# Attention with whole probabilities and a difference of value blocks; score maxima and final roots computed with per-partition scalar columns

## The chip, the cores and the metric

One NeuronCore of a Trainium2 chip runs the whole program. TensorE (PE) does the matrix products and PE transposes, VectorE (DVE) and ScalarE (ACT) work on PSUM and SBUF, GpSimd (POOL) on SBUF, and SyncE (SP) issues the transfers. The metric is device time in microseconds from launch to end; lower is better.

## The reference

A two-layer decoder trunk over 1024 tokens of width 1024. Layer 0 mixes by pooling windows and a short convolution. Layer 1, which the change touches, is sliding-window attention with 16 query heads, 2 key/value heads, a learned sink per head, and blocks of 128 queries. A final RMSNorm follows.

```python
# window 128, blocks of 128 queries; each block sees its own and the previous block of keys
band = (diff >= 0) & (diff < WINDOW)            # diff = i + 128 - j
scores = einsum("bnqkgd,bnskd->bnkgqs", qb, kb) * scale
...
m = maximum(max(scores, -1), sink)
p = exp(scores - m)
p = p / (sum(p, -1) + exp(sink - m))
out = einsum("bnkgqs,bnskd->bnqkgd", p, vb)     # vb = [previous block, own block]
...
h = h + (out * silu(z)) @ w_out + b_out
return h * rsqrt(mean(h * h) + 1e-5) * final_norm_g
```

With a window of 128 and blocks of 128, a query at row i sees exactly 128 keys: the keys j <= i of its own block and the keys j > i of the block before. One 128 x 128 tile of probabilities per head and block thus holds everything: on and below the diagonal stand the own block's keys, above it those of the block before.

## The kernel before

All products are split into a high part (fp32r) and a low rest, so most things exist twice (h and lo, H and L). `split` does that: ACT casts, DVE (or POOL) subtracts.

Layer 0 and the projections of layer 1 run first. The attention then runs as a loop over blocks, `for b in range(NB + 1)`, each with two halves `js` of 8 heads, and the halves of three blocks overlap in it:

- `values(b)` splits block b's values (`vtok[:, b, :]`, in SBUF) into `vp[b]`.
- `queries(b + 1, js)`: ACT casts and POOL subtracts (L936), PE transposes (L939), ACT copies to `qT` (L941).
- `probs(b, js)`: for two groups g of four heads, PE transposes the probabilities `pts` into a PSUM bank (L1058), `split` makes `curH` and `curL` (ACT L179, DVE L180, tile pT), and for b > 0 POOL makes masked copies: `affine_select` L1064 writes the previous block's part to new tiles, L1067 keeps the own block's part in place. That is four selects per group, eight per half.
- `scores(b + 1, js, qT)`: four steps `pair`, each with two heads: PE scores into a bank (L960, L961), DVE merges the two blocks (L966), takes the maxima of both heads (L968), and turns them into the two biases of the exponentials (L969); ACT takes the two exponentials (L972). After the last pair, `norm` computes the sink's part and the reciprocal (L978 to L981) and POOL scales the probabilities (L983).
- `project(b - 1, js)`: 24 products per half with the output weights (L1113 to L1115); the four score steps are spread among them. `summed` adds the residual (L1146), squares (ACT L1147) and multiplies by the final gain (POOL L1150).
- `attend(b, js)`: products of values and probabilities (L1081; for b > 0 eight per half), then ACT L1088, DVE L1089 and L1092, and `split` into aH and aL.
- `finish(b - 1)`: `rsqrt_mean` with n == 1 works on one column: two tensor_scalar (L138), a first guess (L141), and three rounds of L145 and L149, then ACT scales the block (L1129) and it is stored. Its instructions run in the DVE's row during the next block's half js = 0.

PE's order is the program's order. The order on DVE, ACT, POOL and SP in this stage is the one that the scheduler of the language works out at build time. The PSUM banks of scores, transposed queries and transposed probabilities come from one rotation of four buffers (psB).

Of the kernel before, what the change touches and what calls it, by code (L numbers as in the profile page):

```python
# [9 lines left out]
F32 = mybir.dt.float32  # L10
F32R = mybir.dt.float32r
# [3 lines left out]
ALU = mybir.AluOpType  # L15
# [3 lines left out]
P = 128  # L19
# [6 lines left out]
HD = 64  # L26
# [6 lines left out]
WARM = 8  # L33
W_BUFS = 9
T3_BUFS = 14
LEAD = 3
AHEAD = 6
ZLATE = 6
# [40 lines left out]
def trunk(ctx, tc, x, xT, g1, pos, cols, w_in, w_pool, w_out, w_q, w_kv, w_z, b_q, b_kv,  # L79
               sinks, w_o, g_fin, out):  # L80
    nc = tc.nc
    mm, tr = nc.tensor.matmul, nc.tensor.transpose
    act = nc.scalar.activation
    tt, stt, ts = nc.vector.tensor_tensor, nc.vector.scalar_tensor_tensor, nc.vector.tensor_scalar
    ptt = nc.gpsimd.tensor_tensor
# [15 lines left out]
    def psB(dtype=F32):  # L101
# [17 lines left out]
                            compare_op=ALU.is_gt, fill=0.0, base=0, channel_multiplier=-1)  # L119
# [9 lines left out]
    def rsqrt_mean(pool, out_ap, sums, n, part=None):  # L129


        v = pool.tile([P, 8], F32, name="rs_v", bufs=2)[:, :n]
        y = pool.tile([P, 8], F32, name="rs_y", bufs=2)[:, :n]
        a = pool.tile([P, 8], F32, name="rs_a", bufs=2)[:, :n]
        if n == 1:
            h = pool.tile([P, 1], F32, name="rs_h", bufs=2)
            for dst, c in ((v, 1.0), (h, -0.5)):
                ts(out=dst, in0=sums, scalar1=part, scalar2=c / D, op0=ALU.add, op1=ALU.mult)  # L138
        else:
            ts(out=v, in0=sums, scalar1=1.0 / D, scalar2=EPS, op0=ALU.mult, op1=ALU.add)  # L140
        ts(out=y.bitcast(I32), in0=v.bitcast(I32), scalar1=-0.5, scalar2=float(0x5F3759DF),  # L141
           op0=ALU.mult, op1=ALU.add)
        for it in range(3):
            if n == 1:
                stt(out=a, in0=y, scalar=h, in1=y, op0=ALU.mult, op1=ALU.mult)  # L145
            else:
                tt(out=a, in0=y, in1=y, op=ALU.mult)
                stt(out=a, in0=a, scalar=-0.5, in1=v, op0=ALU.mult, op1=ALU.mult)
            stt(out=out_ap if it == 2 else y, in0=a, scalar=1.5, in1=y, op0=ALU.add, op1=ALU.mult)  # L149

    def diag_r(rcol, s):

# [25 lines left out]
    def split(dst_h, dst_l, src, sub=tt):  # L178
        nc.scalar.copy(out=dst_h, in_=src)  # L179
        sub(out=dst_l, in0=src, in1=dst_h.bitcast(F32), op=ALU.subtract)  # L180
# [65 lines left out]
    nsink = const.tile([P, NH], F32, name="nsink")  # L246
# [129 lines left out]
    wraw, wsum, whl, at = {}, {}, {}, {p: i for i, p in enumerate(prods)}  # L376
# [343 lines left out]
    for g in range(4):  # L720
        src = u_pair(g)
        for j in (2 * g, 2 * g + 1):
            if j % 2 and g:
                gated(g, src)
            v = ch_pair(j)
# [20 lines left out]
    if True:  # L746
# [41 lines left out]
        for s in range(2):  # L788
            acc = t2()
            for m in range(8):  # L790
# [5 lines left out]
                for kh in range(2):  # L796
                    w = take()
                    for k in range(KT):
                        f = 8 * kh + k
# [5 lines left out]
                if s == 0 and m == 7:  # L805
# [3 lines left out]
                h, lo = big2(s, F32R), big2(s, F32R)  # L809
                act(out=h, in_=h1, func=AF.Copy, scale=col(C_G2, m))  # L810
                stt(out=lo, in0=h1, scalar=col(C_G2, m), in1=h.bitcast(F32), op0=ALU.mult,
                    op1=ALU.subtract)
# [31 lines left out]
    vtok = keep.tile([P, NB, P], F32, name="vtok")  # L844
# [5 lines left out]
    with tc.tile_pool(name="l1", bufs=2, reuse_waits="tile") as p1:  # L850
# [24 lines left out]
        for b in range(NB):  # L875
            if b + 3 < NB:
# [4 lines left out]
                in1=bkv[:, 0:P], op0=ALU.mult, op1=ALU.add)  # L881
            stt(out=vtok[:, b, :], in0=dst[:, P:256], scalar=rcol1[:, b:b + 1],
                in1=bkv[:, P:256], op0=ALU.mult, op1=ALU.add)
# [13 lines left out]
        for c in range(2):  # L897
            wq = [p for _ in range(4) for p in take(0)]
            for b in range(NB):
# [6 lines left out]
                if c == 0 and 0 < b < 5 or c == 1 and b == 5:  # L906
# [3 lines left out]
                    in1=bq[:, hs(c)], op0=ALU.mult, op1=ALU.add)  # L910
# [34 lines left out]
    def scores(b, js, qT):  # L945

        cols_ = slice(8 * js, 8 * js + 8)
        smax = pe.tile([P, 8], F32, name="smax")
        den = pe.tile([P, 8], F32, name="den")
        res = [pe.tile([P, 4, P], F32, name=f"pt{js}", bufs=2) for _ in range(2)]  # L950
        um = umask.to_broadcast([P, 2, P])

        def pair(g, i2):
            bank = psB()
            bv = bank.rearrange("p (h c) -> p h c", c=256)
            at = 4 * g + 2 * i2
            for i in range(2):
                lq = qT[g][:, (2 * i2 + i) * P:(2 * i2 + i + 1) * P]
                lo, dst = (0, bv[:, i, P:256]) if b == 0 else ((b - 1) * P, bv[:, i, :])
                mm(dst, lhsT=lq, rhs=kT[:, 2 * g, lo:(b + 1) * P], start=True, stop=False)  # L960
                mm(dst, lhsT=lq, rhs=kT[:, 2 * g + 1, lo:(b + 1) * P], start=False, stop=True)  # L961
            if b == 0:
                nc.vector.copy_predicated(out=bv[:, :, P:256], mask=um,
                                          data=neg.unsqueeze(1).to_broadcast([P, 2, P]))
            else:
                nc.vector.copy_predicated(out=bv[:, :, P:256], mask=um, data=bv[:, :, 0:P])  # L966
            m = smax[:, at:at + 2]
            nc.vector.tensor_reduce(out=m, in_=bv[:, :, P:256], axis=AX.X, op=ALU.max)  # L968
            stt(out=m, in0=m, scalar=-0.125, in1=nsink[:, 8 * js + at:8 * js + at + 2],  # L969
                op0=ALU.mult, op1=ALU.min)  # L970
            for i in range(2):
                exps.append(act(  # L972
                    out=res[g][:, 2 * i2 + i, :], in_=bv[:, i, P:256], func=AF.Exp, scale=0.125,
                    bias=smax[:, at + i:at + i + 1], accum_out=den[:, at + i:at + i + 1]))

        def norm():
            es = pe.tile([P, 8], F32, name="es")
            tt(out=es, in0=sink[:, cols_], in1=smax, op=ALU.add)  # L978
            act(out=es, in_=es, func=AF.Exp)
            tt(out=es, in0=den, in1=es, op=ALU.add)  # L980
            nc.vector.reciprocal(out=es, in_=es)  # L981
            for g in range(2):
                ptt(out=res[g], in0=res[g],  # L983
                    in1=es[:, 4 * g:4 * g + 4].unsqueeze(2).to_broadcast([P, 4, P]), op=ALU.mult)

        def last():
            pair(1, 1)
            norm()

        return res, [lambda: pair(0, 0), lambda: pair(0, 1), lambda: pair(1, 0), last]  # L990


# [48 lines left out]
    pa = ctx.enter_context(tc.tile_pool(name="pa", bufs=2, reuse_waits="tile"))  # L1041

    vp = {}

    def values(b):

        t = pa.tile([P, 4, HD], F32R, name="vp", bufs=3)
        v = vtok[:, b, :].rearrange("p (g d) -> p g d", d=HD)
        split(t[:, 0::3, :], t[:, 1:3, :], v)
        vp[b] = t  # L1050

    def probs(b, js):

        terms = []
        for g in range(2):
            bank = psB()
            for i in range(4):
                tr(bank[:, i * P:(i + 1) * P], pts[b, js][g][:, i, :], ident)  # L1058
            curH, curL = (pa.tile([P, 4, P], F32R, name="pT", bufs=9) for _ in range(2))
            split(curH, curL, bank.rearrange("p (h c) -> p h c", c=P))  # L1060
            if b:
                prvH, prvL = (pa.tile([P, 4, P], F32R, name="pT", bufs=9) for _ in range(2))
                for a, t in ((prvH, curH), (prvL, curL)):
                    nc.gpsimd.affine_select(out=a, in_=t.bitcast(F32), pattern=[[0, 4], [-1, P]],  # L1064
                                            compare_op=ALU.is_gt, fill=0.0, base=0,
                                            channel_multiplier=1)
                    nc.gpsimd.affine_select(out=t, in_=t.bitcast(F32), pattern=[[0, 4], [1, P]],  # L1067
                                            compare_op=ALU.is_ge, fill=0.0, base=0,
                                            channel_multiplier=-1)
                terms.append((vp[b - 1], g, prvH, prvL))  # L1070
            terms.append((vp[b], g, curH, curL))
        return terms

    def attend(b, js, terms):
        dst = []
        for g in range(2):
            bank = psA("psA")
            ops = [(v[:, 2 * g:2 * g + 2, :].rearrange("p a d -> p (a d)"), p)
                   for v, gg, h, lo in terms if gg == g for p in (h, lo)]
            for i, (v, p) in enumerate(ops):  # L1080
                mm(bank, lhsT=v, rhs=p, start=(i == 0), stop=(i == len(ops) - 1))  # L1081
            dst.append(bank.rearrange("p (j c) -> p j c", c=P))

        low = pa.tile([P, 4, P], F32, name="pT", bufs=9)
        at = pa.tile([P, 4, P], F32, name="pT", bufs=9)
        for g in range(2):
            own, other = slice(g * HD, (g + 1) * HD), slice((1 - g) * HD, (2 - g) * HD)
            nc.scalar.copy(out=low[own], in_=dst[g][other])  # L1088
            tt(out=at[own], in0=dst[g][own], in1=low[own], op=ALU.add)  # L1089
        s, bb = divmod(b, 4)  # L1090
        for jj in range(2):
            tt(out=at[:, 2 * jj:2 * jj + 2, :], in0=at[:, 2 * jj:2 * jj + 2, :],  # L1092
               in1=sz[4 * s + 2 * js + jj][:, :, bb * P:(bb + 1) * P], op=ALU.mult)
        aH = pa.tile([P, 4, P], F32R, name="aH", bufs=3)
        aL = pa.tile([P, 4, P], F32R, name="aL", bufs=3)
        split(aH, aL, at)
        return aH, aL
# [147 lines left out]
```

## Time and profile before

| what | value |
|---|---|
| median of 3 runs | 1136.29 us (1135.53 to 1137.89) |
| the profiled execution's own time | 1137.09 us |
| its span, first to last instruction | 1135.4 us |
| PE busy | 1078.5 us, 95% |
| DVE busy | 783.5 us, 69% |
| ACT busy | 463.5 us, 41% |
| POOL busy | 224.6 us, 20% |
| granted TensorE clock, mean | 0.995 |

The time is that of the whole launch; the span leaves out 1.7 us around the first and the last instruction. Busy shares are means over the whole program, whose stages differ: the attention loop is the last sixth of it.

### The profile page before, as it was taken

The numbers are of one execution on the slowest core, as the hardware profiler recorded it, in microseconds if no ns is written. First come the engines' busy times: TensorE is split into PE (matmuls) and PEld (weight loads), VectorE is DVE, ScalarE is ACT, GpSimd is POOL, SyncE is SP. The second block draws the span as 40 slices with busy tenths as digits, with TensorE's granted clock in tenths as the row PEclk, the third lists the DMA queues.
The fourth block names the chain that finished last, engine by engine and source line by source line (L and its number), as shares of the span: only waits on it lengthen the run. The fifth ranks groups of instructions, "written<-read, shape, count | busy, mean of one in ns | idle before, by whom it ended". The sixth has DMA issues, their size and how long they took to land.

```text
span 1135.4 us, 14172 instructions
## 1 busy us (share of the span) xinstructions
PE 1078.5 (95%) x5020; PEld 873.1 (77%) x5020; DVE 783.5 (69%) x1392; ACT 463.5 (41%) x961; POOL 224.6 (20%) x396
## 2 busy tenths in 40 slices
PE   4989999999999999999999999999999997898897
PEld 3767788888888888887788788988888885676776
DVE  4699879967696669866645854721143679889995
ACT  4753332423233332334324423320023777777653
POOL 0000000000000000000001010333320226788874
PEclk9999999999999999999999999999999999999999
DMA  5342331221212212126653334410022305370001
GB/s 204 112 167 99 141 128 38 93 84 38 93 38 96 81 56 75 65 75 226 222 203 134 137 142 146 165 38 19 1 93 96 127 24 125 57 93 20 20 20 56
DMA packets 70694, 109.09 MB, mean 96 GB/s; under 512 B 37472, under 2 KB 37600, under 8 KB 70624
## 3 DMA queue, kind: packets, MB, share of 16 engines
q1 hardware_dynamic: 70624, 108.20, 28.9%
q8 instruction: 39, 0.64, 0.2%
q14 instruction: 31, 0.25, 0.1%
HBM read 89.04 MB, written 19.14 MB: 95 GB/s over the span
## 4 chain that ended last, share of the span: by engine, by line
PE 79%; DVE 12%; ACT 5%; issue 2%; DMA 2%; POOL 0%; SPq 0%; DVEq 0%; ACTq 0%
PE b L440 38%; PE psD L801 3%; PE psD L802 3%; PE psA L800 2%; PE psD L800 2%; PE psA L802 2%; PE psA L801 2%; PE psA L186 2%; PE psD L186 2%; PE psA L187 2%; PE psA L188 2%; PE psD L188 2%; PE psD L187 2%; ACT pt L972 1%; DMA W<-w_in 1%
## 5 line engine op out<-in xcount | busy, mean ns | idle before, releaser
L179 ACT CAST W<-W 128x512 fp32r<-128x512 f32 (+1 forms) x199 | 143.9, 731 | 357.9 <-DVE W L180 108.5
L180 DVE TENSOR_TENSOR W<-W 128x512 fp32r<-128x512 f32 (+1 forms) x199 | 162.6, 823 | 115.2 <-ACT W L179 68.6
L690 POOL MEMSET T<- 128x16 f32 x8 | 0.9, 111 | 358.4 <-DVE T L624 229.2
L818 POOL TENSOR_TENSOR t<-t,T 128x512 f32<-128x512 f32 x14 | 19.4, 1387 | 248.5 <-ACT T L817 248.5
L440 PE MATMUL b<-B11h,W 128*128 128x512 f32 x192 | 65.6, 405 | 2.7 <-ACT W L179 1.8
L440 PE MATMUL b<-T2h,W 128*128 128x512 f32 x192 | 64.5, 396 | 2.2 <-ACT W L179 2.2
L440 PE MATMUL b<-B22h,W 128*128 128x512 f32 x192 | 64.7, 398 | 1.2 <-DVE T L469 1.1
L440 PE MATMUL b<-T1h,W 128*128 128x512 f32 x192 | 64.4, 396 | 0.0
L440 PE MATMUL b<-T3h,W 128*128 128x512 f32 x192 | 64.3, 396 | 0.0
L440 PE MATMUL b<-B21h,W 128*128 128x512 f32 x192 | 63.9, 396 | 0.0
L440 PE MATMUL b<-T4h,W 128*128 128x512 f32 x192 | 63.5, 391 | 0.0
L972 ACT ACTIVATE pt<-psB,smax 128x128 f32<-128x128 f32 x128 | 45.4, 366 | 24.8 <-DVE smax L969 19.6
L801 PE MATMUL psD<-U,W 128*128 128x512 f32 x128 | 51.5, 402 | 2.6 <-DVE U L180 2.6
L802 PE MATMUL psA<-U,W 128*128 128x512 f32 x128 | 50.4, 394 | 1.4 <-DVE W L180 1.4
L960 PE MATMUL psB<-kT,qT 128*128 128x256 f32 (+1 forms) x128 | 34.8, 294 | 17.3 <-ACT qT L941 7.6
L802 PE MATMUL psD<-U,W 128*128 128x512 f32 x128 | 50.9, 398 | 0.2 <-DVE W L180 0.2
L800 PE MATMUL psD<-U,W 128*128 128x512 f32 x128 | 51.1, 399 | 0.0
L800 PE MATMUL psA<-U,W 128*128 128x512 f32 x128 | 50.8, 397 | 0.0
L1113 PE MATMUL psD<-O,aH 128*128 128x512 f32 (+1 forms) x128 | 50.7, 396 | 0.0
L801 PE MATMUL psA<-U,W 128*128 128x512 f32 x128 | 50.6, 395 | 0.0
L1115 PE MATMUL psD<-O,aL 128*128 128x512 f32 (+1 forms) x128 | 49.7, 388 | 0.0
L1114 PE MATMUL psD<-O,aH 128*128 128x512 f32 (+1 forms) x128 | 49.6, 387 | 0.0
(330 smaller groups left out, 2923.6 us busy)
## 6 DMA issues: line engine op xcount, KB each, us to landing
W<-w_in SPq DMA_DIRECT2D x54, 512.0 KB, 3.5
W<-w_out SPq DMA_DIRECT2D x32, 512.0 KB, 3.8
W<-w_z SPq DMA_DIRECT2D x16, 512.0 KB, 3.5
O<-o_dram SPq DMA_DIRECT2D x31, 256.0 KB, 5.5
o_dram<-t SPq DMA_DIRECT2D x30, 256.0 KB, 2.0
T<-xT SPq DMA_DIRECT2D x16, 256.0 KB, 4.3
h_dram<-T SPq DMA_DIRECT2D x16, 256.0 KB, 2.1
W<-w_q SPq DMA_DIRECT2D x8, 512.0 KB, 4.4
```

The costliest lines, as they stand in the source:

```text
L179: nc.scalar.copy(out=dst_h, in_=src)
L180: sub(out=dst_l, in0=src, in1=dst_h.bitcast(F32), op=ALU.subtract)
L186: mm(dst, lhsT=ah, rhs=bh, start=(i == 0), stop=False)
L187: mm(dst, lhsT=ah, rhs=bl, start=False, stop=False)
L440: mm(dst, lhsT=w[:, hw, k], rhs=x[hx][:, k], start=start and k + n == 0, stop=k == 3 and n == 2, skip_group_check=not start)
L800: mm(dst, lhsT=w[k][0], rhs=oHL[f][0], start=(f == 0), stop=False)
L801: mm(dst, lhsT=w[k][0], rhs=oHL[f][1], start=False, stop=False)
L802: mm(dst, lhsT=w[k][1], rhs=oHL[f][0], start=False, stop=(f == 15))
L972: exps.append(act(out=res[g][:, 2 * i2 + i, :], in_=bv[:, i, P:256], func=AF.Exp, scale=0.125, bias=smax[:, at + i:at + i + 1], accum_out= ...
L1113: mm(o, lhsT=a[0][:, kk, :], rhs=woH[8 * n + k][:, c], start=(k == 0), stop=False)
L1114: mm(o, lhsT=a[0][:, kk, :], rhs=woL[8 * n + k][:, c], start=False, stop=False)
L1115: mm(o, lhsT=a[1][:, kk, :], rhs=woH[8 * n + k][:, c], start=False, stop=(k == KT - 1))
```

## The change

Three edits:

- `rsqrt_mean` with one column: each of the six steps of the three rounds, a scalar_tensor_tensor whose second tensor is the column y, becomes a tensor_scalar that takes the columns as per-partition scalars.
- `scores`: the one scalar_tensor_tensor over two heads' maxima becomes one tensor_scalar for each head, with the head's column of `nsink` as a per-partition scalar.
- `values`, `probs`: with p the whole tile of probabilities and p_own its masked own part, the output p_prev v[b-1] + p_own v[b] is computed as p v[b-1] + p_own (v[b] - v[b-1]). `values(b)` now also forms and splits the difference for b > 0 (POOL subtracts, then `split`); `probs` keeps the whole h and lo and makes two masked tiles per group (`own`) where it made four.

```diff
         for it in range(3):
+            z = out_ap if it == 2 else y
             if n == 1:
-                stt(out=a, in0=y, scalar=h, in1=y, op0=ALU.mult, op1=ALU.mult)
+                ts(out=a, in0=y, scalar1=y, scalar2=h, op0=ALU.mult, op1=ALU.mult)
+                ts(out=z, in0=a, scalar1=1.5, scalar2=y, op0=ALU.add, op1=ALU.mult)
             else:
                 tt(out=a, in0=y, in1=y, op=ALU.mult)
                 stt(out=a, in0=a, scalar=-0.5, in1=v, op0=ALU.mult, op1=ALU.mult)
-            stt(out=out_ap if it == 2 else y, in0=a, scalar=1.5, in1=y, op0=ALU.add, op1=ALU.mult)
+                stt(out=z, in0=a, scalar=1.5, in1=y, op0=ALU.add, op1=ALU.mult)
...
-            stt(out=m, in0=m, scalar=-0.125, in1=nsink[:, 8 * js + at:8 * js + at + 2],
-                op0=ALU.mult, op1=ALU.min)
             for i in range(2):
+                h = 8 * js + at + i
+                ts(out=m[:, i:i + 1], in0=m[:, i:i + 1], scalar1=-0.125, scalar2=nsink[:, h:h + 1],
+                   op0=ALU.mult, op1=ALU.min)
                 exps.append(act(
...
-        t = pa.tile([P, 4, HD], F32R, name="vp", bufs=3)
-        v = vtok[:, b, :].rearrange("p (g d) -> p g d", d=HD)
-        split(t[:, 0::3, :], t[:, 1:3, :], v)
-        vp[b] = t
+        for i in range(2 if b else 1):
+            v = vtok[:, b, :]
+            if i:
+                v = pa.tile([P, P], F32, name="vd", bufs=1)
+                ptt(out=v, in0=vtok[:, b, :], in1=vtok[:, b - 1, :], op=ALU.subtract)
+            vp[b, i] = t = pa.tile([P, 4, HD], F32R, name=f"vp{i}", bufs=3 - i)
+            split(t[:, 0::3, :], t[:, 1:3, :], v.rearrange("p (g d) -> p g d", d=HD))
...
-            curH, curL = (pa.tile([P, 4, P], F32R, name="pT", bufs=9) for _ in range(2))
-            split(curH, curL, bank.rearrange("p (h c) -> p h c", c=P))
+            h, lo = (pa.tile([P, 4, P], F32R, name="pT", bufs=PT_BUFS) for _ in range(2))
+            split(h, lo, bank.rearrange("p (h c) -> p h c", c=P))
+            terms.append((vp[max(b - 1, 0), 0], g, h, lo))
             if b:
-                prvH, prvL = (pa.tile([P, 4, P], F32R, name="pT", bufs=9) for _ in range(2))
-                for a, t in ((prvH, curH), (prvL, curL)):
-                    nc.gpsimd.affine_select(out=a, in_=t.bitcast(F32), pattern=[[0, 4], [-1, P]],
-                                            compare_op=ALU.is_gt, fill=0.0, base=0,
-                                            channel_multiplier=1)
-                    nc.gpsimd.affine_select(out=t, in_=t.bitcast(F32), pattern=[[0, 4], [1, P]],
+                own = [pa.tile([P, 4, P], F32R, name="pT", bufs=PT_BUFS) for _ in range(2)]
+                for a, t in zip(own, (h, lo)):
+                    nc.gpsimd.affine_select(out=a, in_=t.bitcast(F32), pattern=[[0, 4], [1, P]],
                                             compare_op=ALU.is_ge, fill=0.0, base=0,
                                             channel_multiplier=-1)
-                terms.append((vp[b - 1], g, prvH, prvL))
-            terms.append((vp[b], g, curH, curL))
+                terms.append((vp[b, 1], g, *own))
         return terms
```

`PT_BUFS` is 9, the number that stood there before.

## Rows read from the trace of the kernel before

**Rows 1.** A stretch: length, busy us of PE, PEld, DVE, ACT, POOL; clock, DMA.

```profile
1040.00:1080.00 40.00, 34.97 (x197) 28.02 (x195) 37.22 (x91) 26.88 (x89) 32.76 (x42) 1.00 0.04 14
```

**Rows 2.** Waits from 800 us on, PE's: total us, times, longest us.

```profile
PE psB L960 <- ACT qT L941: 7.6, 10, 2.0
...
PE psB L960 <- DVE smax L969: 5.4, 5, 1.1
...
PE psB L960 <- DVE pT L180: 4.0, 5, 1.4
...
PE psB L1058 <- ACT pt L972: 1.9, 1, 1.9
...
PE psA L1081 <- POOL pT L1064: 1.0, 2, 0.6
...
PE psA L1081 <- POOL pT L1067: 0.9, 1, 0.9
```

**Rows 3.** Timeline of PE in one block: start, duration, and idle before.

```profile
1043.75 2.02 PE L1081 MATMUL psA<-pT,vp 128*128 128x512 f32 x8
...
1049.49 0.39 PE L960 MATMUL psB<-kT,qT 128*128 128x256 f32 x1 [1.17 <-ACT qT L941]
...
1053.43 0.39 PE L960 MATMUL psB<-kT,qT 128*128 128x256 f32 x1 [0.63 <-DVE pT L180]
...
1056.63 0.36 PE L960 MATMUL psB<-kT,qT 128*128 128x256 f32 x1 [1.08 <-DVE smax L969]
...
1058.59 2.02 PE L1081 MATMUL psA<-pT,vp 128*128 128x512 f32 x8
...
1069.89 1.32 PE L1081 MATMUL psA<-pT,vp 128*128 128x512 f32 x5
```

**Rows 4.** Timeline of DVE in the same block.

```profile
1045.00 1.02 DVE L969 SCALAR_TENSOR_TENSOR smax<-smax,nsink 128x2 f32<-128x2 f32 x1
...
1047.79 0.20 DVE L138 TENSOR_SCALAR rs_h<-ss 128x1 f32<-128x1 f32 x1
...
1048.09 0.58 DVE L145 SCALAR_TENSOR_TENSOR rs_a<-rs_y,rs_h 128x1 f32<-128x1 f32 x1
...
1050.03 0.90 DVE L149 SCALAR_TENSOR_TENSOR rs_y<-rs_a,rs_y 128x1 f32<-128x1 f32 x1
1050.85 1.29 DVE L1092 TENSOR_TENSOR pT<-pT,U 128x256 f32<-128x256 f32 x2
```

**Rows 5.** Timeline of POOL in the same block.

```profile
1044.71 1.29 POOL L1150 TENSOR_TENSOR U<-U 128x512 f32<-128x512 f32 x1
1047.62 2.04 POOL L983 TENSOR_TENSOR pt<-pt,es 128x512 f32<-128x512 f32 x2 [1.62 <-ACT psD L1147]
1049.61 1.30 POOL L1150 TENSOR_TENSOR U<-U 128x512 f32<-128x512 f32 x1
```

**Rows 6.** Instructions by line: shortest, median and longest in ns, first and last start.

```profile
L138 DVE TENSOR_SCALAR rs_h<-ss x8: 201/204/204, 969.1 to 1129.3; 128x1 f32<-128x1 f32 x8
...
L145 DVE SCALAR_TENSOR_TENSOR rs_a<-rs_y,rs_h x24: 216/580/870, 969.4 to 1130.7; 128x1 f32<-128x1 f32 x24
...
L149 DVE SCALAR_TENSOR_TENSOR rs_y<-rs_a,rs_y x16: 148/159/903, 971.7 to 1130.5; 128x1 f32<-128x1 f32 x16
```

**Rows 7.** Groups by line and shape from 860 us on: busy us, mean ns, idle before.

```profile
L1064 POOL TENSOR_SCALAR_AFFINE_SELECT pT<-pT 128x512 fp32r<-128x512 f32 x56 | 41.9, 752 | 6.5 <-ACT pT L179 6.5
...
L936 POOL TENSOR_TENSOR qs<-U,qs 128x256 fp32r<-128x256 f32 x30 | 25.3, 846 | 58.5 <-ACT qs L935 58.5
...
L969 DVE SCALAR_TENSOR_TENSOR smax<-smax,nsink 128x2 f32<-128x2 f32 x64 | 19.8, 310 | 0.9
...
L145 DVE SCALAR_TENSOR_TENSOR rs_a<-rs_y,rs_h 128x1 f32<-128x1 f32 x24 | 11.8, 491 | 0.4
...
L149 DVE SCALAR_TENSOR_TENSOR rs_y<-rs_a,rs_y 128x1 f32<-128x1 f32 x16 | 6.9, 432 | 0.4
...
L180 DVE TENSOR_TENSOR vp<-vtok,vp 128x128 fp32r<-128x128 f32 x8 | 3.1, 395 | 0.0
```

More of the change, by code (lines that the diff above doesn't have):

```diff
@@ L35 @@
 T3_BUFS = 14
+PT_BUFS = 9
 LEAD = 3
@@ L1082, in attend @@
             dst.append(bank.rearrange("p (j c) -> p j c", c=P))
-        low = pa.tile([P, 4, P], F32, name="pT", bufs=9)
-        at = pa.tile([P, 4, P], F32, name="pT", bufs=9)
+        low = pa.tile([P, 4, P], F32, name="pT", bufs=PT_BUFS)
+        at = pa.tile([P, 4, P], F32, name="pT", bufs=PT_BUFS)
         for g in range(2):
```

## The prediction

> **What bounds the kernel now.** I read the page first: PE is busy 95% of the span, so a change that takes no PE work away can only win what PE waits, and the three edits leave every matmul in place. The busy time by stretch then shows where PE waits at all. Up to the attention loop it is full. In the loop, [rows 1], PE has 35.0 of 40 us, DVE 37.2 and POOL 32.8: the engine that comes nearest to being full is DVE, and POOL, which is 20% busy over the whole span, is at 82% here. The clock is 1.00, so nothing is lost to it.
>
> The chain of waits says for whom PE waits. From 800 us on, the six that the change can touch add up to 20.8 us [rows 2]; two more, of 1.7 and 0.3 us, are left out. Most are one line, the scores matmul L960, which needs either the transposed queries from ACT or a PSUM bank that DVE has to empty. Two rows are waits of the value products for POOL's selects. These 20.8 us are the most that it can win, and some of it, a wait behind a table load of ACT, it can't reach.
>
> The timeline of one block shows where in the block they lie [rows 3]. From the first value products to the next ones, 1043.75 to 1058.59, takes 14.84 us and holds three gaps, 1.17, 0.63 and 1.08, together 2.88 us. The other half, 1058.59 to 1069.89, takes 11.30 us with almost the same matmuls. The difference is `finish`: its column arithmetic runs on DVE in the long half only.
>
> What DVE does there [rows 4, 5]: the step rs_a on one column starts at 1048.09 and ends at 1048.67, just as the first of POOL's two L983 ends (1047.62 plus half of 2.04 is 1048.64). The step rs_y ends at 1050.93, and POOL's L1150 at 1050.91. L969, two elements per partition, takes 1.02 us and ends at 1046.02, with the other L1150 ending at 1046.00. So a DVE instruction that reads two tensors from SBUF waits for the POOL instruction that is running. Across all executions [rows 6] L145 takes 216 ns at the least and 580 in the median, L149 148 at the least and 903 at the most. The tensor_scalar L138 on the same kind of column, with one tensor, took 201 to 204 ns in all eight, that at 1047.79 in the midst of L983.
>
> **The column edits.** Per block six steps of the root chain change form. They cost 3 x 0.491 + 3 x 0.432 = 2.77 us now [rows 7], the last step taken like the two before it. The new forms are not in the trace. With one scalar column tensor_scalar took 204 ns; a second column costs an estimated 68 more, the distance of L145's shortest, which has one, to L149's, which has none (216 less 148) [rows 6]. So 3 x 0.272 + 3 x 0.204 = 1.43 us, a saving of 1.34. Not all of it is kept: behind rs_y stands L1092 [rows 4], which reads two SBUF tensors too, and would itself wait for L1150 until 1050.9. I keep 0.95, between 0.6 (the long rs_y gives nothing) and 1.34.
>
> L969: 64 instructions of 310 ns become 128 of 204: 26.1 us for 19.8 [rows 7], 0.1 us more per pair, so +0.4 per half. In return the first exponential needs only the first of the two, and none waits for POOL. At the start of the long half that is worth up to 1.02 - 0.16 = 0.86 us, on the way to ACT's copies of the queries, the first gap. But L978, the next in DVE's row, reads two SBUF tensors and would meet the same L1150, unless POOL is done with it earlier. With fewer selects before it, it should be: I take 0.75, between 0 and 0.86.
>
> The Trainium skill has a rule against this edit: "VectorE: DVE Perf Modes", section "Rules for kernel authors", says to keep the number of chained DVE instructions low. Its fixed part of 58 cycles would make an estimated 4 us of the 64 added instructions; by the trace's 204 ns they are 13 us before what the shorter waits give back, so the row is the harsher judge.
>
> **The value edit.** POOL loses 56 selects, 41.9 us [rows 7], and gains 7 subtractions of 128x128, bounded above by the 0.85 us of L936 with twice the elements, below by half of it: 3 to 6 us. Per half that is 4 selects, 3 us less of POOL in its 11 to 15. What follows on DVE: fewer meetings. One meeting cost 0.3 to 0.7 above, so I take 0.4 per half, between 0 and 0.8. On PE: the value products take the whole probabilities first, which wait for no select, and the waits for POOL, 1.0 + 0.9 us [rows 2], go; at worst they stay.
>
> What it adds: per block from the second on, one ACT cast, one DVE subtraction of 0.395 us (the vp row of [rows 7]), one POOL subtraction. The cast stands beside ACT's idle time in the long half and costs nothing while the POOL subtraction is ready; if not, the second rival. The DVE subtraction lies in the long half: +0.4. Nothing is moved past a transfer: SP's row is untouched.
>
> **The sum.** Long halves: -0.95 (chain) - 0.75 (start) - 0.4 (meetings) + 0.2 (half of L969's 0.4, as the first exponential leaves earlier) + 0.4 (value subtraction) = -1.5 us each. The bounds are -0.6 + 0.4 + 0.4 = +0.2 and -(1.34 + 0.86 + 0.8) + 0.4 = -2.6; the gaps allow 2.9. Five halves have such gaps (the chains that begin near 969, 996, 1022, 1048 and 1074 us): -7.5. The value products' waits: -1.9 (0 to -1.9). The transposes that waited 1.9 us for exponentials behind a locked L969 (L1058 in [rows 2]): -0.5 (0 to -1). Short halves: PE is the bound there, DVE's extra 0.4 shows as +0.1: +0.5 (0 to +2). The last chain, after the last matmul, has no POOL beside it for five of its six steps: 3 x (0.272 - 0.216) + 3 x (0.204 - 0.148) = +0.3. Together -9.1, from +3.3 to -15.
>
> The profiled execution took 1137.1 us, which gives 1128.0; the median of the runs is 0.8 below it, which gives 1127.2. I say 1127.5. About 0.2%, 2.3 us, is what a measurement of this kernel can tell from no change.
>
> **The rivals.**
>
> *The lock only moves.* What rs_y and L969 waited for, L978, L1092 and aL behind them wait for instead; or the columns are held up like the tensors. Then the -1.7 of chain and start vanish, the meetings' -0.4 stands against +0.6 of new work in each of five halves (+1.0), the exponentials' -0.5 goes, and -1.9 at the value products, +0.5 and +0.3 stay: about 0, or 1136. For it speaks that POOL runs without a pause behind L983 [rows 5]; against it, the eight L138.
> The Trainium skill bears on this: "SBUF — State Buffer", section "Who interferes with whom", lets a DVE instruction with one SBUF input pass GpSimd, but counts tensor_scalar among those that may enter a two-port mode and then be held. By the first clause the columns go free, by the second they wait as now. L138's 201 to 204 ns agree with the first.
>
> *A new wait on ACT* (slower). ACT's cast of the difference stands in its row before the casts of probabilities and the exponentials, and waits for POOL's subtraction. If that is queued behind the two L983, ACT stands 2.04 us per block, seven times 14.3, against the 9.1 won: +5, about 1142. It decides from 1.3 us per block (9.1 / 7). For it: POOL's row is full in that half. Against it: the values were ready hundreds of us earlier, so POOL can subtract whenever its row has a place.
>
> *All gaps close.* If DVE stops being the bound, all of [rows 2] but the part behind the table load goes, some 19 us: 1118. For it: the short half shows PE alone as bound at 11.30 us. Against it: DVE keeps over 90% of its work.
>
> **How the numbers follow.** The forecast 0.60, its own range 1121 to 1133; all gaps close 0.15; the lock moves 0.13; the ACT wait 0.12. Faster by over 0.2%: 0.75; within: 0.13; slower: 0.12. The range for 8 in 10 reaches from 1118 (the gaps all close) to 1138 (the lock moves, with the upper bound of the unknown costs), and leaves out the ACT wait and the far ends.
>
> **What would show it.** Right: L145 and L149 on one column near 270 and 200 ns in every execution, whatever POOL does; L969 at 204, 128 times; POOL near 26 of 40 us late in the loop; no wait of L1081 for POOL; the long half near 13.3 us, the short one unchanged; the gap before L960 that ends with ACT qT below 0.5. Wrong: L1092, L978 or aL longer by what L149 and L969 lost; an ACT wait for POOL's difference; a different order of DVE's row that puts the probabilities' L180 behind more than it has before it now, which no row of this trace can exclude.

## The result, and the profile after

The changed kernel takes 1124.7 us in the median (1124.5 to 1124.77) against 1135.92 us, a ratio of 0.9898 with an interval of 0.988 to 0.9915: 11.2 us faster. The forecast was 1127.5, faster. The profiled execution spans 1122.8 us (1135.4 before). PE has as many matmuls as before, 5020; of the 12.6 us, 9.4 are time in which it stood idle (56.9 us before, 47.5 now).

The lines of the changed kernel differ: the root's steps are L147 and L148, the maxima L974, the sink's sum L982, the sum for the denominator L984, the selects L1075, the value products L1088, ACT's low part L1095, the gate multiplications L1099, the gain L1157, `split` L182 and L183.

First the stretch that answers to [rows 1], in the same columns.

```profile
1040.00:1080.00 40.00, 36.89 (x209) 29.91 (x206) 36.77 (x109) 29.88 (x95) 26.55 (x31) 1.00 0.07 28
```

POOL went from 32.8 to 26.6 us, PE from 35.0 to 36.9, and DVE is about as full as before: it does the same in less time. All of PE's named waits from 800 us on, to be read beside [rows 2]:

```profile
PE psB L963 <- ACT qT L944: 7.3, 9, 3.1
PE psB L963 <- DVE pT L183: 2.8, 5, 0.8
PE psB L963 <- DVE smax L974: 1.5, 1, 1.5
PE psA L1088 <- DVE smax L974: 1.4, 1, 1.4
PE psB L1068 <- ACT pt L976: 0.2, 1, 0.2
```

13.2 us are left, of 22.8 with the two that the prediction left out. PE's value products wait for no select any more. The timeline of PE over one block, as in [rows 3]:

```profile
1036.68 2.02 PE L1088 MATMUL psA<-pT,vp 128*128 128x512 f32 x8
...
1041.43 0.38 PE L963 MATMUL psB<-kT,qT 128*128 128x256 f32 x1 [0.50 <-ACT qT L944]
...
1045.32 0.39 PE L963 MATMUL psB<-kT,qT 128*128 128x256 f32 x1 [0.58 <-DVE pT L183]
...
1049.16 2.00 PE L1088 MATMUL psA<-pT,vp 128*128 128x512 f32 x8
...
1053.76 0.39 PE L963 MATMUL psB<-kT,qT 128*128 128x256 f32 x1 [0.35 <-ACT qT L944]
...
1060.65 2.00 PE L1088 MATMUL psA<-pT,vp 128*128 128x512 f32 x8
```

The long half is 12.48 us (14.84), the third gap is gone, and the short half is 11.49 (11.30). What DVE and POOL do in it, as in [rows 4, 5]:

```profile
1037.73 0.33 DVE L974 TENSOR_SCALAR smax<-smax,nsink 128x1 f32<-128x1 f32 x2
...
1039.62 1.22 DVE L984 TENSOR_TENSOR es<-den,es 128x8 f32<-128x8 f32 x1
...
1042.44 0.27 DVE L147 TENSOR_SCALAR rs_a<-rs_y,rs_h 128x1 f32<-128x1 f32 x1
1042.63 1.78 DVE L1099 TENSOR_TENSOR pT<-pT,U 128x256 f32<-128x256 f32 x2
1044.34 0.20 DVE L148 TENSOR_SCALAR rs_y<-rs_a,rs_y 128x1 f32<-128x1 f32 x1
```

```profile
1039.53 1.29 POOL L1157 TENSOR_TENSOR U<-U 128x512 f32<-128x512 f32 x1 [1.71 <-ACT psD L1154]
1041.22 2.04 POOL L987 TENSOR_TENSOR pt<-pt,es 128x512 f32<-128x512 f32 x2 [0.40 <-DVE rs_y L142]
```

The columns pass POOL: L147 runs in the midst of the two L987. The lock, as the prediction calls it (a DVE instruction with two SBUF tensors is held until the POOL instruction that is running ends), has not gone; it has found others. L984, eight columns wide, takes 1.22 us and ends at 1040.84 as L1157 does at 1040.82. The pair L1099 took 1.29 us in [rows 4] and takes 1.78. By line (shortest, median, longest ns), as in [rows 6], and by shape (busy us, mean ns), as in [rows 7]:

```profile
L147 DVE TENSOR_SCALAR rs_a<-rs_y,rs_h x24: 255/272/275, 966.9 to 1118.0; 128x1 f32<-128x1 f32 x24
...
L148 DVE TENSOR_SCALAR rs_y<-rs_a,rs_y x16: 199/202/214, 967.7 to 1117.7; 128x1 f32<-128x1 f32 x16
...
L974 DVE TENSOR_SCALAR smax<-smax,nsink x128: 191/203/215, 894.4 to 1085.7; 128x1 f32<-128x1 f32 x128
```

```profile
L1075 POOL TENSOR_SCALAR_AFFINE_SELECT pT<-pT 128x512 fp32r<-128x512 f32 x56 | 42.1, 770 | 9.4 <-ACT pT L182 7.2 <-DVE pT L183 2.2
...
L1099 DVE TENSOR_TENSOR pT<-pT,U 128x256 f32<-128x256 f32 x32 | 23.3, 767 | 0.2
...
L984 DVE TENSOR_TENSOR es<-den,es 128x8 f32<-128x8 f32 x16 | 7.6, 477 | 4.4 <-ACT es L983 4.1
...
L1056 POOL TENSOR_TENSOR vd<-vtok 128x128 f32<-128x128 f32 x7 | 3.2, 459 | 16.3 <-DVE es L982 13.3 <-DVE vp L183 3.0
...
L183 DVE TENSOR_TENSOR vp<-vd,vp 128x128 fp32r<-128x128 f32 x7 | 1.9, 278 | 0.0
```

### The profile page after: what moved, and what is told of

The parts are those of the page before. It is cut to its first block, busy times and chain, and to the rows that moved or that the text cites. A ratio compares the mean times of both kernels' runs of the same rounds, so it can differ in the third digit from the quotient of the medians.

```text
span 1122.8 us, 14175 instructions
## 1 busy us (share of the span) xinstructions
PE 1075.3 (96%) x5020; PEld 873.4 (78%) x5020; DVE 777.1 (69%) x1463; ACT 464.4 (41%) x968; POOL 191.6 (17%) x347
## 4 chain that ended last, share of the span: by engine, by line
PE 83%; DVE 10%; ACT 4%; issue 2%; DMA 1%; SPq 0%; POOL 0%; DVEq 0%; ACTq 0%; POOLq 0%
PE b L443 39%; PE psD L805 3%; PE psD L804 3%; PE psA L805 3%; PE psA L804 2%; PE psD L803 2%; PE psA L803 2%; PE psA L189 2%; PE psD L189 2%; PE psA L191 2%; PE psA L190 2%; PE psD L191 2%; PE psD L190 2%; PE psD L1122 2%; PE psD L1121 1%
## 5 line engine op out<-in xcount | busy, mean ns | idle before, releaser
L182 ACT CAST W<-W 128x512 fp32r<-128x512 f32 (+1 forms) x199 | 144.0, 730 | 357.4 <-DVE W L183 108.9
L183 DVE TENSOR_TENSOR W<-W 128x512 fp32r<-128x512 f32 (+1 forms) x199 | 162.7, 823 | 114.7 <-ACT W L182 67.9
L1122 PE MATMUL psD<-O,aL 128*128 128x512 f32 (+1 forms) x128 | 49.7, 388 | 0.0
L1121 PE MATMUL psD<-O,aH 128*128 128x512 f32 (+1 forms) x128 | 49.6, 387 | 0.0
L443 PEld LDWEIGHTS b<-B11h,W 128*128 128x128 f32 x192 | 36.7, 192 | 12.3 <-ACT W L182 2.3
```

Source lines behind the costliest of these rows:

```text
L443: mm(dst, lhsT=w[:, hw, k], rhs=x[hx][:, k], start=start and k + n == 0, stop=k == 3 and n == 2, skip_group_check=not start)
L1121: mm(o, lhsT=a[0][:, kk, :], rhs=woL[8 * n + k][:, c], start=False, stop=False)
L1122: mm(o, lhsT=a[1][:, kk, :], rhs=woH[8 * n + k][:, c], start=False, stop=(k == KT - 1))
```

## The experiments

Twelve kernels, each timed against the kernel before on the same chip. Before the attention loop, where nothing differs, profiled executions differ among themselves by up to 2.3 us. So the table also gives the loop of the profiled execution: from the second query transposes of the loop (927.69 us in the kernel before, 927.79 in the changed one) to the end of the span. It is one execution each; the ratio is the verdict. The last column counts the stretches of that loop, up to its last matmul, in which TensorE's granted clock fell to 0.50, the 1.2 GHz level. Each lasted 3.4 us, so it gives up an estimated 1.7 us of PE's work.

| kernel | median us | ratio, interval | loop us | clock drops |
|---|---|---|---|---|
| before | 1135.91 to 1136.81 | 1 | 207.7 | 0 |
| changed | 1124.7 | 0.9898 (0.988 to 0.9915) | 195.0 | 0 |
| root columns alone | 1135.85 | 0.9994 (0.9984 to 1.0003) | 206.7 | 2 |
| maxima columns alone | 1134.46 | 0.998 (0.9967 to 0.9993) | 206.2 | 2 |
| value edit alone | 1130.98 | 0.9952 (0.9939 to 0.9964) | 203.3 | 2 |
| both columns | 1128.54 | 0.9928 (0.9916 to 0.9941) | 199.6 | 1 |
| changed + POOL load | 1123.97 | 0.989 (0.9869 to 0.9912) | 195.7 | 2 |
| changed, own parts first | 1125.5 | 0.9897 (0.9877 to 0.9917) | 195.4 | 0 |
| changed, no difference | 1122.22 | 0.9876 (0.9855 to 0.9897) | 194.7 | 0 |
| changed + output in PSUM | 1113.39 | 0.9791 (0.9768 to 0.9814) | 184.6 | 0 |
| the same + sink part in PSUM | 1115.93 | 0.9819 (0.9794 to 0.9845) | 187.5 | 1 |
| changed + load + own first | 1126.77 | 0.9904 (0.9879 to 0.993) | 199.5 | 2 |
| before + output in PSUM | 1123.96 | 0.9885 (0.9863 to 0.9908) | 196.1 | 1 |
| both columns + output in PSUM | 1123.17 | 0.9877 (0.9853 to 0.99) | 193.3 | 2 |

Where in the loop, from transposes to transposes: the front up to the first long half, the five long halves, the four short ones between them, and the end.

| kernel | front | long x5 | short x4 | end |
|---|---|---|---|---|
| before | 41.2 | 71.0 | 46.7 | 48.8 |
| root columns alone | 41.2 | 63.6 | 50.5 | 51.3 |
| maxima columns alone | 39.6 | 68.0 | 48.1 | 50.5 |
| both columns | 39.6 | 60.9 | 49.5 | 49.6 |
| changed | 38.0 | 60.1 | 49.1 | 47.8 |
| changed + output in PSUM | 35.7 | 56.4 | 45.8 | 46.7 |

One thing varies in these kernels beside the edit: the scheduler lays the rows of DVE, ACT and POOL anew. From 900 us on DVE has 466 instructions in the kernel before; 430 of them stand in the same order with the root columns, 383 with the output in PSUM, 360 with both columns. Between the changed kernel and the one with own parts first or with the POOL load, the order on DVE is the same but for at most three instructions. No run here held the order fixed and changed the form alone, so what a difference of order does to the times stays open.

### One edit at a time

The root columns alone are the first hunk of the change put into the kernel before; the maxima alone the second, the value edit the third, the fourth run the first two.

> The kernel before with the root chain's column edit alone. Theory (a DVE instruction with one SBUF tensor is not held by POOL, and most of that time is kept): the six steps go from 2.77 to 1.43 us per chain and five long halves keep about 0.95 us each, less 0.3 us at the tail: 4 to 5 us faster than before. Rival (the lock only moves to L1092 and to the subtraction of aL behind them): within 1 us of before. Either way the column steps should take 255 to 275 and 200 to 215 ns in every execution, although POOL is as full as before.

> The kernel before with the maxima's column edit alone. Theory: the first gap of the long halves shrinks only if the held instruction behind L969 (the sum for the sink, L978) is free earlier too, and POOL's row is as full as before here, so 1 to 3 us faster. Rival (the lock moves to L978): 0 to 2 us slower, because 64 instructions more run on DVE. The sink's sum should then have a mean well above the 263 ns of before.

> The kernel before with the value edit alone (half the selects, the difference of the values). Theory by the prediction's terms: -1.9 us for the value products' waits, -0.4 for fewer meetings and +0.4 for the added subtraction in each long half: about 2 us faster. Rival (POOL's row is what holds the columns, so that thinning it does most of the work): 6 us faster or more, with L145 and L149 on one column falling from 491 and 432 ns to below 350.

> The kernel before with both column edits and the old selects: the changed kernel without its value edit. Theory: 5 to 8 us faster, the sum of the two alone, and the whole change's 11.2 us needs the value edit for the rest. Rival (POOL's row decides): less than 3 us faster, since the tensors behind the columns wait for POOL instead.

The root columns alone give nothing that can be told, though their steps do what was expected: 21.8 us of DVE time ([rows 7], and 3.1 us for the last step) become 11.4. A part of the 10.4 went to other instructions, as the groups by shape of that kernel show, and one row of the kernel before that stands nowhere above:

```profile
L1094 DVE TENSOR_TENSOR pT<-pT,U 128x256 f32<-128x256 f32 x32 | 25.8, 844 | 0.2
...
L971 DVE SCALAR_TENSOR_TENSOR smax<-smax,nsink 128x2 f32<-128x2 f32 x64 | 23.6, 369 | 0.8
```

```profile
L1092 DVE TENSOR_TENSOR pT<-pT,U 128x256 f32<-128x256 f32 x32 | 20.1, 667 | 0.2
```

The gate multiplications took 5.7 us more, the maxima 3.8 (19.8 in [rows 7]): 9.5 us came back on these two lines. Other lines took less, so that is not the whole account. Busy time over the whole loop, the kernel before and then this one, in the columns of [rows 1]:

```profile
927.69:1135.40 207.71, 177.24 (x981) 142.86 (x979) 177.39 (x421) 136.22 (x412) 149.01 (x184) 0.99 0.27 54
```

```profile
926.22:1132.90 206.68, 180.97 (x981) 144.72 (x979) 174.13 (x421) 137.23 (x412) 148.39 (x184) 0.98 0.27 54
```

DVE is busy 3.3 us less and PE stands idle 4.8 us less (30.5 to 25.7), but the same matmuls keep PE busy 3.7 us longer. The long halves shrank by 7.4 us; the short ones grew by 3.9 and the end by 2.5, and in each of these two lies a drop of the clock, together an estimated 3.4 us. The one in the first short half came at the end of a wait of PE for ACT of 2.60 us. In the end DVE was early and POOL was not, so PE stood in the value products: rows of its timeline, then of busy time by the microsecond.

```profile
1099.89 0.39 PE L1083 MATMUL psA<-pT,vp 128*128 128x512 f32 x1
1101.48 3.86 PE L1083 MATMUL psA<-pT,vp 128*128 128x512 f32 x7 [1.20 <-POOL pT L1066]
```

```profile
1102.00:1103.00 1.00, 0.91 (x3) 0.37 (x2) 0.00 (x0) 0.48 (x2) 1.00 (x3) 1.00 0.00 0
1103.00:1104.00 1.00, 0.91 (x3) 0.34 (x2) 0.61 (x1) 0.36 (x1) 1.00 (x3) 0.57 0.89 369
1104.00:1105.00 1.00, 1.00 (x3) 0.65 (x3) 0.07 (x1) 0.00 (x0) 0.48 (x1) 0.50 0.38 156
```

After the pause and two microseconds of products in pieces the granted clock fell to 0.50. That both drops are common in this kernel is not shown; over all its timed executions the mean clock was 0.993, against 0.994 for the kernel before.

The maxima alone give 1.7 us, inside what was expected. The sink's sum rose only to 317 ns from 263, but the sum behind it from 166 to 395. Both together give 7.6 against 2.0 for the sum of the two alone (by the loop 8.1 against 2.5). In the long halves, where the prediction put them, the two do add up: -7.4 and -3.0 alone, -10.1 together. The excess lies in the short halves and the end, where each edit alone has two drops of the clock in its profiled execution and both together have one; the rest of it is not explained. Neither theory of the first run survives unchanged: the lock does move, as the rival said, but only in part, and the long halves keep their gain. The value edit alone gives 5.2 us, more than its terms and less than the rival's 6, and L145 and L149 stayed at 510 and 460 ns, so it did not work through the columns.

### What in the value edit counts

The load: after `own`, two selects of half width for each whole tile into a small tile. Own first: `terms` gets the own parts before the whole ones. No difference: `vp[b, 1]` is replaced by `vp[b, 0]`, so this kernel leaves the difference out of its result too.

```diff
+                for t in (h, lo):
+                    for u in (t[:, 0:2], t[:, 2:4]):
+                        junk = pa.tile([P, 2, P], BF16, name="junk", bufs=1)
+                        nc.gpsimd.affine_select(out=junk, in_=u.bitcast(F32), ...
...
-            terms.append((vp[max(b - 1, 0), 0], g, h, lo))
+            whole = (vp[max(b - 1, 0), 0], g, h, lo)
...
                 terms.append((vp[b, 1], g, *own))
+            terms.append(whole)
...
-                terms.append((vp[b, 1], g, *own))
+                terms.append((vp[b, 0], g, *own))
```

> The changed kernel with POOL's time given back: for each whole tile two more selects of half the width into a tile that nothing reads, in the place where the previous block's selects stood (the output is unchanged). Theory (the value edit wins by POOL's shorter row: fewer meetings with DVE and own parts that are ready sooner): most of the 3.5 to 4 us that the value edit adds to the two column edits goes, the time is 1127 to 1129 us, and the tensor instructions that read two SBUF tensors get longer. Rival (it wins because the value products begin with tiles that wait for no select): 1124 to 1126 us, as that order is kept.

> The changed kernel with the terms of the value products in the other order: the masked own parts first, the whole probabilities last. Theory (POOL's row is short enough now that the own parts are ready): within 1.5 us of the changed kernel. Rival (the order of the terms is what removed PE's waits for POOL): those waits come back, 2 us or more slower than the changed kernel.

> The changed kernel without the difference of the values: the own parts are multiplied with the own block's values, so one POOL subtraction, one ACT cast and one DVE subtraction per block are left out, and with them that part of the computation. By the prediction's term these cost 0.4 us in each of five long halves: 1.5 to 2.5 us faster than the changed kernel. Rival (they lie in time that no one waits for): within 0.7 us of it.

> The changed kernel with both: POOL's time given back, with the extra selects ahead of the own parts, and the own parts first in the value products. Apart from the in-place select this stands as the old selects did. Theory (the value edit won by own parts that no longer stand behind POOL's other work when PE begins the products; either a shorter POOL row or the new order of the terms does it): the waits of the value products for POOL come back with 2 us or more, and the time is that of both column edits alone, 1127 to 1130 us. Rival (the gain was a chance of the order on DVE): 1123 to 1126 us, as in the two runs with one of them.

With its load given back POOL was busy 38.2 of 40 us between 1040 and 1080, and the time did not rise; nor did the gate multiplications get longer (768 ns for 767), and aL got shorter (711 for 866). The theory that a shorter POOL row wins falls. The steady long halves even took 11.4 us for 12.5, while the front and the first short half grew by 1.8 and 1.6 us, with a drop of the clock in each. With the own parts first the time did not rise either, so the order of the terms alone is not it. With both, the products' waits for POOL came back:

```profile
PE psA L1095 <- POOL pT L1081: 4.0, 8, 0.9
```

and the loop was 199.5 us, that of both columns without the value edit (199.6), though not in the same parts: its steady long halves are those of the changed kernel (12.4 for 12.5), and it loses in the first two long halves (25.4 for 22.6), the first short one and the end, with a drop of the clock in each of the last two. The ratio, 0.9904, lies too near to tell it from the changed kernel's 0.9898, so this rests on the waits and on one execution's loop. Read that way, the value edit wins because PE's value products no longer stand behind POOL, and either a short row or work that needs no select is enough; that is argued, not shown. The difference itself costs next to nothing: without it the loop is 0.3 us shorter and its long halves are the same to 0.02 us. Of the rest of its profiled execution's gain, 2.3 us lie before the loop, where the changed kernel's clock stood at 0.50 from 534.4 to 537.8 us and this one's at 1.00.

### Taking the tensors out of SBUF

The attention output is kept in the bank of the products instead of an SBUF tile:

```diff
-        at = pa.tile([P, 4, P], F32, name="pT", bufs=PT_BUFS)
+        at = dst[0]
```

> The changed kernel with the attention output kept in the PSUM bank of the value products, where ACT's low part is added, instead of an SBUF tile: the two gate multiplications and the subtraction of aL then read one tensor from SBUF and one from PSUM, the same operations otherwise. Theory (what counts is the number of SBUF tensors): the gate multiplications fall from 767 ns in the mean and 1516 at the most to below 450 in every execution, aL from 866 to below 720, and the time falls by 2 to 5 us to about 1121. Rival (the lock moves to what is left, the sink's sums, or PE is the bound by now): the same durations, but within 1.5 us of the changed kernel.

> The kernel before, none of the change, with the attention output kept in PSUM. Theory (every held instruction ahead of PE's waits must go before the gaps close; the root's and the maxima's steps are still held): 4 to 8 us faster than before, and those steps as long as before or longer. Rival (the gate multiplications were most of it all along): 12 us faster or more.

> Both column edits and the attention output in PSUM, with the old selects: all of the best kernel but the value edit. Theory: PE then waits for POOL's selects, in the first and the last blocks above all, and the time is 3 to 5 us above the best kernel so far, 1116 to 1119 us. Rival (the value edit is worth nothing once DVE is free): within 1.5 us of 1113.4.

On the changed kernel this gave another 11 us, more than twice what was expected. The operations are the same; one operand, and for the sums and the gate multiplications the output, lies elsewhere. The gate multiplications by line, in the kernel before and then, with two more lines, in that kernel:

```profile
L1092 DVE TENSOR_TENSOR pT<-pT,U x32: 409/423/1508, 929.7 to 1119.2; 128x256 f32<-128x256 f32 x32
```

```profile
L1099 DVE TENSOR_TENSOR psA<-psA,U x32: 418/431/433, 928.1 to 1094.5; 128x256 f32<-128x256 f32 x32
...
L183 DVE TENSOR_TENSOR aL<-psA,aH x16: 676/683/693, 930.9 to 1095.6; 128x512 fp32r<-128x512 f32 x16
...
L984 DVE TENSOR_TENSOR es<-den,es x16: 148/167/1217, 900.9 to 1075.0; 128x8 f32<-128x8 f32 x16
```

With one operand out of SBUF none is held; L984, which still reads two tensors there, still is. The Trainium skill, "SBUF — State Buffer", section "Who interferes with whom", says that a DVE instruction with two SBUF inputs contends with a GpSimd instruction that reads SBUF and that one with at most one SBUF input, outside the two-port modes, does not: both halves agree with these rows. POOL gained too: its selects L1075, the same work, fell from 770 to 636 ns in the mean and from 1101 to 652 at the most. The lock works both ways: each of the twelve selects of more than 0.9 us in the changed kernel began while DVE subtracted two SBUF tensors (eleven times aL) and ended 0.49 to 0.50 us after that subtraction. The edit also leaves one tile per half out of the rotation of nine pT buffers and changes DVE's order. No wait in the two traces shows an instruction short of a pT buffer, but how much of the 11 us these two make was not tried.

In the kernel before, the same line gave 12.0 us, as much as the whole change; 4 to 8 were expected. The rival was right, at its edge: the gate multiplications and the aL behind them were where most of the held time that mattered stood, and the columns remained held (L145 490 ns). Without the value edit the best kernel loses nearly all it had won over the changed one, 1123.17 against 1113.39, where 3 to 5 us were expected; the waits of PE for POOL are back in that kernel:

```profile
PE psA L1084 <- POOL pT L1067: 3.2, 2, 1.9
...
PE psA L1084 <- POOL pT L1070: 0.9, 1, 0.9
```

They are 4.1 us, and the granted clock was 0.96 in the stretches 920 to 960 and 960 to 1000 us that hold them: two drops, an estimated 3.4 of the 8.7 us by which this loop is longer. The value edit is worth 5.2 us on the kernel before, 3.8 behind both columns and 9.8 here; both columns are worth 7.6 us on the kernel before, but with the output in PSUM and the old selects only 0.8 (1123.96 to 1123.17).

One step further, ACT wrote the sink's exponential into the last scores bank:

```diff
-            act(out=es, in_=es, func=AF.Exp)
-            tt(out=es, in0=den, in1=es, op=ALU.add)
+            ep = bk[-1][:, 0:8]
+            act(out=ep, in_=es, func=AF.Exp)
+            tt(out=es, in0=den, in1=ep, op=ALU.add)
```

> The kernel of the last run before this one (attention output in PSUM) with one more SBUF tensor taken away: ACT writes the exponential of the sink's part into the dead part of the last scores bank, so that the sum for the denominator reads one tensor from SBUF. Theory (each held instruction in front of PE's waits counts): the sum falls from 298 ns in the mean to below 180 in every execution, the long halves from 11.2 to 10.9 us, the time by 1 to 2 us to about 1112. Rival (PE is the bound): no change beyond 0.7 us.

The sum fell to 153 ns, and the kernel is 2.5 us slower than without it: its fastest execution took 1115.5 us, the other's slowest 1114.82. The long halves take 57.5 us for 56.4 (10.9 each was expected), and the first short half 14.92 for 13.17, with a drop of the clock. PE has a new wait, by far the longest of that kernel, since the transposes of the probabilities need the bank that the sum now holds:

```profile
PE psB L1072 <- DVE es L988: 6.8, 7, 1.7
```

The best version is thus the changed kernel with the output in PSUM, 1113.39 us, 2.1% faster than before.

## Why the prediction was right

**The sizes of the new instructions** held: 272 and 204 ns were worked out for the columns, 268 and 205 measured (means), 203 for the maxima. So did POOL's 26 of 40 us, the products' waits that went, and the last chain's loss: from the last value products to the end of the span it is 20.65 us for 20.45.

**Long halves.** -7.5 us was said, -10.9 measured (71.0 to 60.1). The mechanism held: of the three gaps of 2.88 us the third closed and 1.08 us is left. The term of the maxima was right, -0.75 and +0.2 a half for -0.6 measured alone. That of the chain was too small: 0.95 was kept, between 0.6 and 1.34, and the root columns alone shortened each long half by 1.5, more than all the time that the steps themselves gave back. Why is not known; DVE's order changed with them. The rival that the lock only moves was given as a matter of yes or no; the runs show it in part. The gate multiplications, whose line the prediction had named as a sign of being wrong, took 3.2 us more (20.1 to 23.3) and the sum L984 4.9 (2.7 to 7.6), while the sink's sum and aL, which it had named too, took less; the gain came all the same.

**Short halves.** +0.5 us was said, +2.4 measured, 2.0 of it in the first two of them (13.18 to 14.21 and 10.87 to 11.88 us). In the first, PE's wait for ACT's copies, behind a table load, is 3.07 us where it was 2.04: the whole 1.03. "PE is the bound there" was thus not right: PE waits in them, and with the output in PSUM the steady ones take 10.86 us, for 11.30 before and 11.49 in the changed kernel with the same columns. So the columns alone do not make them long; and the root columns, without any added maxima, made them 3.9 us longer.

**Value edit.** -1.9 for the products' waits was the right mechanism and too small: 3.8 to 4.6 us (both columns against the changed kernel, by medians and by the loop), in the front and the end above all; up to an estimated 1.7 of the 4.6 is a drop of the clock that only the first of the two has. The -0.4 per half for fewer meetings is not there: the four lines that still read two SBUF tensors in every half took 49.7 us with both columns and 48.6 in the changed kernel, 0.1 a half. The +0.4 for the difference falls with the run without it. That these two errors cancelled was luck.

**The sum.** Front and end fell by 4.2 us where the terms for them make -2.1, the long halves by 3.4 more than was said, and the short ones took 1.9 of it back. By the loop that is -12.7 for -9.1, by medians -11.2: part of the nearness is errors of opposite sign. A slip that does not bear on it: the lower end of the added bounds is -15.6, not -15.

**The rivals.** The ACT wait did not come: no row shows ACT waiting for the difference, 0.459 us on POOL. All gaps closed in no version of the change alone; with the output in PSUM PE's waits at L963 fell to 3.6 us and the time went below the range, as that rival's mechanism says.

## What to carry to other kernels

List every DVE instruction that reads two SBUF tensors beside a busy POOL, with its longest and its median, before costing the removal of one: part of the wait goes to the next in the row, so what removing one is worth depends on which others remain. Before calling an edit worthless, split the time by stretch and look at the granted clock: here the root columns won 7.4 us in the long halves, and an estimated 3.4 us of the loss elsewhere was two drops of the clock. Often the cheapest cure is to leave an operand in PSUM, but a bank kept longer is a wait for whoever needs it. As DVE gets faster, look for what PE stands behind next; here, with the output in PSUM, it was POOL's masks.

## What the hardware showed unexpectedly

A tensor_tensor of 128x256 with one operand and the output in PSUM takes 431 ns, against 423 from SBUF to SBUF when nothing holds it: PSUM cost nothing here. A second scalar column adds some 66 ns to a tensor_scalar of one element (202 to 204, then 268 to 272).

A POOL that is 95% busy (38.2 of 40 us) did not slow the steady blocks. How long PE stood does not by itself say whether the granted clock falls: in the changed kernel PE waited 3.07 us before 982.90 and the stretch around it, 981 to 984 us, shows a clock of 1.00 with 1.10 us of busy PE. At the same place the clock fell to 0.50 at the end of a wait of 2.60 us with the root columns alone, and 0.8 to 1.2 us after one of 1.87 with the maxima alone and one of 2.91 with both.
